# Two gates of a decoder trunk: three 256-column products per weight tile, one bank per chunk, and a last tile emptied in two halves

## The chip, the cores and the metric

The kernel runs on one core of one Trainium2 chip. A core has a matmul engine (TensorE, PE in the profile, with its weight loads as PEld), a vector engine (VectorE, DVE), a scalar engine (ScalarE, ACT), a general one (GpSimd, POOL) and a queue for transfers (SyncE, SP). The metric is device time in microseconds (us). Three runs of the kernel before took 669.51, 670.52 and 673.18 us; the median is 670.52.

## What is computed

Two layers of a decoder on 256 tokens with 1024 features, in f32. Each layer has a mixer (attention), a squared-ReLU MLP, and at its end a gate, which is what the change touches:

```python
for i in range(DEPTH):                      # DEPTH = 2
    hn = rms_norm(h, mix_norm[i])
    h = h + mixer_i(hn)                     # even or odd mixer
    u = jax.nn.relu(rms_norm(h, ff_norm[i]) @ w_ff1[i])
    h = h + (u * u) @ w_ff2[i]
    g = jax.nn.sigmoid(rms_norm(h, ple_norm[i]) @ w_ple_gate[i])
    h = h + g * (p[i] @ w_ple_proj[i])
return h
```

## The kernel before

The residual `h` lies in SBUF with features on the partitions: 8 row tiles of 128 features by 256 tokens. A `Norm` object holds the input of a product: row tiles of `h` times the norm's gain, split into a high part (`hi`, rounded for a fast matmul mode, made by ScalarE, L248) and a low rest (`lo`, VectorE, L249). The factor 1/rms of a token isn't in it: it is found beside the product from the sum of squares (`square`, `cols`) and multiplied in at the end, as `rb` in the gate.

Weights come in 1 MB tiles, in the order of `plan`, into three buffers (`raw`). Each tile is split in four pieces into `hi` (ScalarE, L182) and `lo` (VectorE, L184), ahead of its use. These pieces have a low priority for the scheduler that orders each engine's instructions (`LATER`), and it sets them between the other work of ScalarE and VectorE. A product is then three: high by high, low x by high weight, high x by low weight.

A gate has 4 chunks of 256 output columns; a chunk is two column tiles of 128, each with 8 row tiles of weights, so a gate has 64 weight tiles. `wide_mm` (L312, L314) takes a weight tile's high part against the 512 columns of [hi | lo] of x, into two halves of a bank, and its low part against the 256 columns of hi. The two halves are added afterwards: a ScalarE copy (L622) and a VectorE addition (L623). Then come the product with `rb` (L624), the sigmoid (L626), the product with the embedding projection (L627), the addition to `h` (L628), and either the split of `h` for the next layer or, at the program's end, a transfer to the output (L630). Other products, such as the output projection, go through `feat_mm` (L299): three matmuls of 256 columns for each weight tile, added up in one place of the bank.

Behind the gate of layer 0 stands the q/k/v projection of layer 1 (`tok_units`, L330): for each of 8 row tiles of x, six matmuls of 512 columns, with x as the loaded operand and four row tiles in a weight tile.

Of the kernel before, what the change touches and what calls it, by code (L numbers as in the profile page):

```python
# [8 lines left out]
F32 = mybir.dt.float32  # L9
FR = mybir.dt.float32r  # L10
I32 = mybir.dt.int32
AF = mybir.ActivationFunctionType
# [3 lines left out]
P = 128  # L16
S = 256
# [4 lines left out]
ZB = 7  # L22
# [30 lines left out]
def trunk(ctx, tc, xT, pT, pos, cst, vec, w_c, w_kv, w_dil, w_uq, w_ukv, w_eo,  # L53
          w_odd, w_oo, w_f1, w_f2, w_g, w_p, out):
    nc = tc.nc
# [6 lines left out]
    tp = ctx.enter_context(tc.tile_pool(name="tp", bufs=2))  # L62
    sp = ctx.enter_context(tc.tile_pool(name="sp", bufs=3))
    pm = ctx.enter_context(tc.tile_pool(name="pm", bufs=4, space=PS))
    pa = ctx.enter_context(tc.tile_pool(name="pa", bufs=2, space=PS))
    pt = ctx.enter_context(tc.tile_pool(name="pt", bufs=2, space=PS))

    V, A, T, G = nc.vector, nc.scalar, nc.tensor, nc.gpsimd
# [4 lines left out]
    h = cp.tile([P, KD, S], F32, name="h")  # L73
# [71 lines left out]
    class Weights:  # L145
# [56 lines left out]
        def take(self, ahead=True):  # L202
            while len(self.ready) <= self.taken or (self.rest and self.rest[0][0] == self.taken):
                self.piece()
            if not self.rest:
                self.flush()
            self.taken += 1
            if ahead:
                self.pump(99)
            return self.ready[self.taken - 1]  # L210

    weights = Weights()
    take, pump = weights.take, weights.pump
# [76 lines left out]
    def passes(xh, xl, wh, wl):  # L290
        return ((wh, xh), (wh, xl), (wl, xh))

    def feat_mm(ps, n, wt, x, k0, nk, total, done):

        (wh, wl), (xh, xl) = wt, x
        for kk in range(nk):
            for j in range(n):
                for i, (a, b) in enumerate(passes(xh, xl, wh, wl)):
                    T.matmul(ps[:, j, :], lhsT=a[:, kk, j * P:(j + 1) * P],  # L299
                             rhs=b[:, k0 + kk, :],  # L300
                             start=(done == 0 and kk == 0 and j == 0 and i == 0),
                             stop=(done + kk == total - 1 and i == 2),
                             skip_group_check=True)

    def wide_mm(ps, j, wt, x, nk, done=True, first=True):


        wh, wl = wt
        sl = slice(j * P, (j + 1) * P)
        for kk in range(nk):  # L310
            last = done and kk == nk - 1
            T.matmul(ps, lhsT=wh[:, kk, sl], rhs=x[:, kk], start=(first and kk == 0),  # L312
                     stop=last, skip_group_check=True)
            T.matmul(ps[:, 0, :], lhsT=wl[:, kk, sl], rhs=x[:, kk, 0, :], start=False,  # L314
                     stop=last, skip_group_check=True)

    def wide_first(pss, wt, x):

        for kk in range(8):
            for j, ps in enumerate(pss):  # L320
                wide_mm(ps, j, (wt[0][:, kk:kk + 1], wt[1][:, kk:kk + 1]), x[:, kk:kk + 1], 1,
                        kk == 7, kk == 0)
# [282 lines left out]
        down(3)  # L605

    def gate(n_g, es, nxt):
        rb = None
        for c in range(4):
            wt = take()  # L610
            pool, tag = (pa, "s") if c == 2 else (pm, "mm")
            pss = [pool.tile([P, 2, S], F32, tag=tag, name="g") for _ in range(2)]
            if c == 0:
                wide_first(pss, wt, n_g.x)
            for j, ps in enumerate(pss):
                k = 2 * c + j
                if c > 0:
                    wide_mm(ps, j, wt, n_g.x, 8)
                if rb is None:
                    rb = n_g.cols()  # L620
                t = tp.tile([P, S], F32, tag="z", name="t", bufs=ZB)
                A.activation(t, ps[:, 1, :], AF.Copy)  # L622
                V.tensor_add(t, ps[:, 0, :], t)  # L623
                V.tensor_mul(t, t, rb)  # L624
                g = tp.tile([P, S], F32, tag="sq", name="g")
                A.activation(g, t, AF.Sigmoid)  # L626
                V.tensor_mul(g, es[k // 4][:, k % 4, :], g)  # L627
                V.tensor_add(h[:, k, :], h[:, k, :], g)  # L628
                if nxt is None:
                    nc.sync.dma_start(out[:, k, :], h[:, k, :])  # L630
                else:
                    nxt.split(k)
            if nxt is not None:
                nxt.square(c)


    def rope_angles():
# [189 lines left out]
    with tc.manual_schedule():  # L827
# [3 lines left out]
        pss = [pm.tile([P, 512], F32, tag="mm", name="mm") for _ in range(2)]  # L831
        wts = [weight_tiles([P, 4, 416]) for _ in range(2)]
        for k in range(8):
# [6 lines left out]
            sl = slice(k % 4, k % 4 + 1)  # L840
# [10 lines left out]
        wh, wl = take(False)  # L851
# [7 lines left out]
        for k in range(8):  # L859
            if k == 4:  # L860
                wh, wl = take(False)
            tok_mm(psk, 256, (wh[:, k % 4:k % 4 + 1], wl[:, k % 4:k % 4 + 1]), x0, k, 1, 8, k)
    with tc.manual_schedule(engines={mybir.EngineType.PE}):
# [46 lines left out]
        es, pss = [], []  # L910
# [29 lines left out]
    mlp(0, nf, ng)  # L940
    n1 = Norm(V_MIX + 8)
    gate(ng, es, n1)


# [32 lines left out]
    with tc.manual_schedule(engines={mybir.EngineType.PE}):  # L977
        run(group(0))
        for g in range(2):
            if g == 0:  # L980
                dense, units = group(1), [3, 3, 3, 3, 3]
            else:
                es, pss = [], []
# [8 lines left out]
    ng = Norm(V_PLE + 8)  # L992
    mlp(1, nf, ng)
    gate(ng, es, None)


# [86 lines left out]
```

## Time and profile before

| | |
|---|---|
| median of three runs | 670.52 us |
| profiled execution | 670.03 us |
| its span, first to last instruction | 668.0 us |
| TensorE busy | 653.2 us (98%) |
| VectorE busy | 524.5 us (79%) |
| ScalarE busy | 471.9 us (71%) |
| mean granted TensorE clock | 0.998 |
| gate of layer 0 | about 310.0 to 333.2 us |
| gate of layer 1 | about 639.3 to 662.5 us |

The shares are means over the whole span. The ends of matmuls are modelled, so the distance from start to start tells what one costs. An engine that isn't on the path may be slower or faster without effect; it matters where another engine waits for it.

### The profile page before, as it was taken

To read this page: it belongs to the slowest core of one execution; us is meant where nothing else is said; L and a number is where in the kernel's file an instruction comes from. 1 tells how busy PE (TensorE), PEld (TensorE's weight loads), DVE (VectorE), ACT (ScalarE), POOL (GpSimd) and SP (SyncE) were. 2 spreads that over 40 slices of the span, in tenths; PEclk is the share of its full clock that TensorE was granted. 3 is DMA by queue.
4 is the path that set the end of the run, shared out by engine and by line. 5 is a ranking of instruction groups with operands and counts; after the bars stand their busy time and mean duration, and the time that the engine had idled before them with its cause. 6 is when DMAs were issued, how large, how long until landed. Compare 5 with 4: busy or idle time off the path is not lost.

```text
span 668.0 us, 10798 instructions
## 1 busy us (share of the span) xinstructions
PE 653.2 (98%) x3862; PEld 564.3 (84%) x3862; DVE 524.5 (79%) x1307; ACT 471.9 (71%) x1118; POOL 12.9 (2%) x38
## 2 busy tenths in 40 slices
PE   9999999999999999999989999999999999999996
PEld 8888778988888888888868777888888888888885
DVE  5799787697787787889988686666977878778996
ACT  6968886599858658557864775766986585785663
POOL 3110000000000000000000000000000000000000
PEclk9999999999999999999999999999999999999999
DMA  7756413156546455455345433331754564554511
GB/s 232 277 195 243 181 64 127 64 178 240 191 164 219 163 190 217 164 177 187 119 189 212 172 130 138 121 127 64 266 199 173 186 213 171 211 187 172 187 57 63
DMA packets 19493, 114.08 MB, mean 171 GB/s; under 512 B 2288, under 2 KB 5488, under 8 KB 6640
## 3 DMA queue, kind: packets, MB, share of 16 engines
q1 hardware_dynamic: 19440, 113.40, 47.8%
q8 instruction: 30, 0.49, 0.3%
q14 instruction: 23, 0.19, 0.1%
HBM read 112.34 MB, written 1.05 MB: 170 GB/s over the span
## 4 chain that ended last, share of the span: by engine, by line
PE 88%; DVE 7%; ACT 2%; DMA 2%; issue 1%; SPq 1%; ACTq 0%
PE f L312 34%; PE f L314 18%; PE mm L330 16%; PE mm L299 7%; PE g L312 3%; PE g L314 2%; PE tr L419 2%; DVE lo L184 1%; DVE x L249 1%; PE tr L339 1%; PE s L389 1%; PE o L428 1%; PE s L387 1%; DMA raw<-w_kv 1%; DVE acc L260 1%
## 5 line engine op out<-in xcount | busy, mean ns | idle before, releaser
L184 DVE TENSOR_TENSOR lo<-raw,hi 128x512 fp32r<-128x512 f32 (+1 forms) x400 | 266.2, 690 | 57.5 <-ACT hi L182 57.1
L182 ACT ACTIVATE hi<-raw 128x512 fp32r<-128x512 f32 (+1 forms) x400 | 234.8, 629 | 100.9 <-PE f L312 60.7
L312 PE MATMUL f<-x,hi 128*128 128x512 f32 x512 | 178.3, 392 | 0.0
L312 PE MATMUL f<-u,hi 128*128 128x512 f32 x512 | 177.8, 391 | 0.0
L314 PE MATMUL f<-x,lo 128*128 128x256 f32 x512 | 143.4, 280 | 0.0
L314 PE MATMUL f<-u,lo 128*128 128x256 f32 x512 | 143.4, 280 | 0.0
L312 PEld LDWEIGHTS f<-x,hi 128*128 128x128 f32 x512 | 95.8, 187 | 21.3
L312 PEld LDWEIGHTS f<-u,hi 128*128 128x128 f32 x512 | 95.7, 187 | 21.0
L330 PE MATMUL mm<-hi,x 128*128 128x512 f32 (+1 forms) x320 | 105.5, 398 | 0.2 <-ACT hi L121 0.2
L314 PEld LDWEIGHTS f<-x,lo 128*128 128x128 f32 x512 | 96.8, 189 | 0.0
L314 PEld LDWEIGHTS f<-u,lo 128*128 128x128 f32 x512 | 96.8, 189 | 0.0
L330 PEld LDWEIGHTS mm<-hi,x 128*128 128x128 f32 x320 | 61.1, 191 | 13.5 <-issue 1.8
L330 PE MATMUL mm<-lo,x 128*128 128x512 f32 (+1 forms) x160 | 63.2, 395 | 3.3 <-DVE lo L184 3.3
L299 PE MATMUL mm<-x,hi 128*128 128x256 f32 x256 | 48.3, 289 | 0.0
L576 DVE TENSOR_TENSOR u<-sq,u 128x256 fp32r<-128x256 f32 x64 | 26.7, 420 | 26.7 <-ACT u L575 26.7
L312 PE MATMUL g<-x,hi 128*128 128x512 f32 x128 | 44.5, 392 | 0.0
L299 PEld LDWEIGHTS mm<-x,hi 128*128 128x128 f32 x256 | 39.5, 190 | 3.7 <-issue 3.0
L330 PEld LDWEIGHTS mm<-lo,x 128*128 128x128 f32 x160 | 30.6, 191 | 10.3 <-DVE lo L184 4.2
L314 PE MATMUL g<-x,lo 128*128 128x256 f32 x128 | 36.2, 283 | 0.0
L299 PE MATMUL mm<-x,lo 128*128 128x256 f32 x128 | 36.1, 282 | 0.0
L248 ACT ACTIVATE x<-h,vc 128x256 fp32r<-128x256 f32 x48 | 22.8, 501 | 14.3 <-DVE h L595 9.6
L401 ACT ACTIVATE pr<-sc,nm 128x128 f32<-128x128 f32 x64 | 27.5, 447 | 7.4 <-DVE nm L396 7.3
(195 smaller groups left out, 843.6 us busy)
## 6 DMA issues: line engine op xcount, KB each, us to landing
raw<-w_f SPq DMA_DIRECT2D x64, 1024.0 KB, 4.7
raw<-w_odd SPq DMA_DIRECT2D x12, 1024.0 KB, 4.7
raw<-w_g SPq DMA_DIRECT2D x8, 1024.0 KB, 4.7
raw<-w_dil SPq DMA_DIRECT2D x6, 1024.0 KB, 4.9
raw<-w_eo SPq DMA_DIRECT2D x4, 1024.0 KB, 4.8
raw<-w_oo SPq DMA_DIRECT2D x4, 1024.0 KB, 5.0
raw<-w_p SPq DMA_DIRECT2D x2, 1024.0 KB, 4.8
raw<-w_c SPq DMA_DIRECT2D x8, 208.0 KB, 4.2
```

Of the source, the lines that this page charges most:

```text
L182: A.activation(hi, raw, AF.Copy)
L184: self.low = lambda: V.tensor_sub(lo, raw, hi.bitcast(F32))
L248: A.activation(self.hi[:, k, :], h[:, k, :], AF.Copy, scale=g)
L249: V.scalar_tensor_tensor(self.lo[:, k, :], h[:, k, :], g, self.hi[:, k, :].bitcast(F32), op0=OP.mult, op1=OP.subtract)
L260: V.tensor_add(self.acc, self.acc, sq)
L299: T.matmul(ps[:, j, :], lhsT=a[:, kk, j * P:(j + 1) * P], rhs=b[:, k0 + kk, :], start=(done == 0 and kk == 0 and j == 0 and i == 0), stop= ...
L312: T.matmul(ps, lhsT=wh[:, kk, sl], rhs=x[:, kk], start=(first and kk == 0), stop=last, skip_group_check=True)
L314: T.matmul(ps[:, 0, :], lhsT=wl[:, kk, sl], rhs=x[:, kk, 0, :], start=False, stop=last, skip_group_check=True)
L330: T.matmul(pss[t][:, :n], lhsT=a[:, k0 + kk, t * P:(t + 1) * P], rhs=b[:, kk, :], start=(done + kk == 0 and i == 0), stop=(done + kk == to ...
L401: A.activation(prs[i][:, sl], scs[i][:, sl], AF.Exp, scale=-1.0, bias=nms[i][:, t:t + 1], **kw)
L419: T.transpose(ps[:, i * P:(i + 1) * P], pr[:, i * P:(i + 1) * P], ident)
L576: V.tensor_sub(ul, sq, uh.bitcast(F32))
```

## The change

Both gates call `feat_mm` with both column tiles of a chunk in one bank, so the high and low products are added by TensorE itself. Copy and addition fall away; product with `rb`, sigmoid, product and addition to `h` run once per chunk on 512 elements of a partition. The split for the next layer follows per chunk (`pair`). In the last gate the fourth chunk is done tile by tile, and its second tile is emptied in two halves of 128 tokens, each with its own transfer.

```diff
     def gate(n_g, es, nxt):
+        x = (n_g.hi, n_g.lo)
         rb = None
         for c in range(4):
-            wt = take()
-            pool, tag = (pa, "s") if c == 2 else (pm, "mm")
-            pss = [pool.tile([P, 2, S], F32, tag=tag, name="g") for _ in range(2)]
-            if c == 0:
-                wide_first(pss, wt, n_g.x)
-            for j, ps in enumerate(pss):
-                k = 2 * c + j
-                if c > 0:
-                    wide_mm(ps, j, wt, n_g.x, 8)
+            wh, wl = take()
+            last = c == 3 and nxt is None
+            for a, b in ((0, 1), (1, 2)) if last else ((0, 2),):
+                n = b - a
+                sl = slice(a * P, b * P)
+                pool, tag = (pa, "s") if c % 2 else (pm, "mm")
+                ps = pool.tile([P, 2, S], F32, tag=tag, name="g")[:, :n, :]
+                feat_mm(ps, n, (wh[:, :, sl], wl[:, :, sl]), x, 0, 8, 8, 0)
                 if rb is None:
-                    rb = n_g.cols()
-                t = tp.tile([P, S], F32, tag="z", name="t", bufs=ZB)
-                A.activation(t, ps[:, 1, :], AF.Copy)
-                V.tensor_add(t, ps[:, 0, :], t)
-                V.tensor_mul(t, t, rb)
-                g = tp.tile([P, S], F32, tag="sq", name="g")
-                A.activation(g, t, AF.Sigmoid)
-                V.tensor_mul(g, es[k // 4][:, k % 4, :], g)
-                V.tensor_add(h[:, k, :], h[:, k, :], g)
-                if nxt is None:
-                    nc.sync.dma_start(out[:, k, :], h[:, k, :])
-                else:
-                    nxt.split(k)
+                    rb = n_g.cols()[:, None, :]
+                halves = ((0, P), (P, S)) if last and a else ((0, S),)
+                for u, v in halves:
+                    t = tp.tile([P, 2, S], F32, tag="z", name="t", bufs=ZB)[:, :n, :v - u]
+                    V.tensor_mul(t, ps[:, :, u:v], rb[:, :, u:v].to_broadcast([P, n, v - u]))
+                    g = tp.tile([P, 2, S], F32, tag="sq", name="g")[:, :n, :v - u]
+                    A.activation(g, t, AF.Sigmoid)
+                    k = 2 * (c % 2) + a
+                    V.tensor_mul(g, es[c // 2][:, k:k + n, u:v], g)
+                    hp_ = h[:, 2 * c + a:2 * c + b, u:v]
+                    V.tensor_add(hp_, hp_, g)
+                    if nxt is None:
+                        nc.sync.dma_start(out[:, 2 * c + a:2 * c + b, u:v], hp_)
             if nxt is not None:
-                nxt.square(c)
+                nxt.pair(c)
```

The scheduler's order on VectorE changes with it. At the end of layer 0's gate it was this before (lo_3874 is the low part of layer 1's first weight tile, lo_3943 of its second; g, t and h are the gate's, x_3723 is layer 1's input):

```order
L628 TENSOR_TENSOR h_84<-h_84,g_3933 128x256
L249 SCALAR_TENSOR_TENSOR x_3723<-h_84,vc_82,x_3723 128x256
L623 TENSOR_TENSOR t_3998<-g_3955,t_3998 128x256
L184 TENSOR_TENSOR lo_3874<-raw_3728,hi_3873 128x512
L249 SCALAR_TENSOR_TENSOR x_3723<-h_84,vc_82,x_3723 128x256
L260 TENSOR_TENSOR acc_3724<-acc_3724,sq_3939 128x512
L627 TENSOR_TENSOR g_3976<-ple_1082,g_3976 128x256
L624 TENSOR_TENSOR t_3998<-t_3998,cr_3774 128x256
L628 TENSOR_TENSOR h_84<-h_84,g_3976 128x256
L184 TENSOR_TENSOR lo_3943<-raw_3807,hi_3942 128x512
L627 TENSOR_TENSOR g_4002<-ple_1082,g_4002 128x256
L249 SCALAR_TENSOR_TENSOR x_3723<-h_84,vc_82,x_3723 128x256
```

Two rows further on there, behind another L628, stands the last piece of lo_3874. Now the third chunk's work (t_3944, g_3946) reads as follows, with lo_3884 as the low part of layer 1's first weight tile and lo_3958 of its second:

```order
L184 TENSOR_TENSOR lo_3884<-raw_3728,hi_3883 128x512
L249 SCALAR_TENSOR_TENSOR x_3723<-h_84,vc_82,x_3723 128x256 x2
L184 TENSOR_TENSOR lo_3884<-raw_3728,hi_3883 128x512
L249 SCALAR_TENSOR_TENSOR x_3723<-h_84,vc_82,x_3723 128x256 x2
L260 TENSOR_TENSOR acc_3724<-acc_3724,sq_3880 128x512
L624 TENSOR_TENSOR t_3944<-g_3895,cr_3789 128x512
L184 TENSOR_TENSOR lo_3884<-raw_3728,hi_3883 128x512
L184 TENSOR_TENSOR lo_3958<-raw_3812,hi_3957 128x512
L628 TENSOR_TENSOR g_3946<-ple_1082,g_3946 128x512
L184 TENSOR_TENSOR lo_3884<-raw_3728,hi_3883 128x512
L630 TENSOR_TENSOR h_84<-h_84,g_3946 128x512
L184 TENSOR_TENSOR lo_3958<-raw_3812,hi_3957 128x512 x2
```

All four pieces of layer 1's first weight tile now stand ahead of the third chunk's addition to `h`, where the last of them stood behind the last chunk's. On ScalarE, at the last chunk of the same gate, the order is now this (hi_4048 is the high part of layer 1's third weight tile, g_4020 the last chunk's sigmoid):

```order
L248 ACTIVATE x_3723<-h_84,vc_82 128x256 x2
L259 ACTIVATE sq_3954<-h_84 128x512
L182 ACTIVATE hi_4048<-raw_3886 128x512 x4
L626 ACTIVATE g_4020<-t_4018 128x512
L248 ACTIVATE x_3723<-h_84,vc_82 128x256 x2
```

The third tile's four pieces stand in front of the last sigmoid. At the program's end VectorE empties the last two column tiles so:

```order
L624 TENSOR_TENSOR t<-g,cr 128x256
L628 TENSOR_TENSOR g<-ple,g 128x256
L630 TENSOR_TENSOR h<-h,g 128x256
L624 TENSOR_TENSOR t<-g,cr 128x128 x2
L628 TENSOR_TENSOR g<-ple,g 128x128 x2
L630 TENSOR_TENSOR h<-h,g 128x128 x2
```

Each step is done for both halves before the next step begins; before, each tile had L623, L624, L627 and L628 on 256 columns.

## Rows read from the trace of the kernel before

**Rows 1.** Busy us by stretch: PE, PEld, DVE, ACT, POOL; clock, DMA share, GB/s:
```profile
310.00:333.20 23.20, 23.20 (x134) 20.37 (x133) 21.58 (x53) 18.54 (x42) 0.00 (x0) 1.00 0.38 136
333.20:340.00 6.80, 3.53 (x16) 2.38 (x14) 6.80 (x18) 5.68 (x14) 0.00 (x0) 1.00 0.00 0
639.30:662.50 23.20, 23.19 (x133) 20.09 (x131) 20.27 (x49) 13.03 (x29) 0.00 (x0) 1.00 0.11 35
```
**Rows 2.** Waits of TensorE, whole run: us in total, times, longest:
```profile
PE mm L330 <- DVE lo L184: 3.3, 2, 2.0
```
**Rows 3.** Timeline of TensorE, gate of layer 1 (start, duration), 20 tiles apart:
```profile
646.72 0.40 PE L312 MATMUL g<-x,hi 128*128 128x512 f32 x1
...
653.66 0.39 PE L312 MATMUL g<-x,hi 128*128 128x512 f32 x1
```
**Rows 4.** Timeline of TensorE, output projection of layer 1, 13 tiles apart:
```profile
455.05 0.40 PE L299 MATMUL mm<-x,hi 128*128 128x256 f32 x2
...
459.73 0.40 PE L299 MATMUL mm<-x,hi 128*128 128x256 f32 x2
```
**Rows 5.** Timeline of TensorE, q/k/v projection of layer 1, nine matmuls apart:
```profile
361.02 0.39 PE L330 MATMUL mm<-lo,x 128*128 128x512 f32 x1
...
363.06 0.39 PE L330 MATMUL mm<-lo,x 128*128 128x512 f32 x1
```
**Rows 6.** Groups of VectorE from 310 to 340: busy us, mean ns, idle before:
```profile
L623 DVE TENSOR_TENSOR t<-g,t 128x256 f32<-128x256 f32 x8 | 3.3, 418 | 0.5 <-ACT t L622 0.5
L624 DVE TENSOR_TENSOR t<-t,cr 128x256 f32<-128x256 f32 x8 | 3.2, 418 | 0.0
```
**Rows 7.** Groups of ScalarE from 310 to 340:
```profile
L182 ACT ACTIVATE hi<-raw 128x512 fp32r<-128x512 f32 x20 | 12.2, 630 | 2.5 <-PE g L312 2.1 <-ACT sq L259 0.5
...
L626 ACT ACTIVATE g<-t 128x256 f32<-128x256 f32 x8 | 3.2, 414 | 0.0
L622 ACT ACTIVATE t<-g 128x256 f32<-128x256 f32 x8 | 3.0, 378 | 1.2 <-PE g L314 1.2
```
**Rows 8.** Timeline of VectorE around the end of layer 0's gate:
```profile
321.95 1.09 DVE L624 TENSOR_TENSOR t<-t,cr 128x256 f32<-128x256 f32 x3
...
334.89 0.68 DVE L184 TENSOR_TENSOR lo<-raw,hi 128x512 fp32r<-128x512 f32 x1
...
339.17 1.28 DVE L184 TENSOR_TENSOR lo<-raw,hi 128x512 fp32r<-128x512 f32 x2
```
**Rows 9.** Timeline of TensorE at the start of layer 1, waits in brackets:
```profile
333.23 0.39 PE L330 MATMUL mm<-hi,x 128*128 128x512 f32 x1
335.63 0.50 PE L330 MATMUL mm<-lo,x 128*128 128x512 f32 x1 [2.01 <-DVE lo L184]
...
339.90 0.50 PE L330 MATMUL mm<-lo,x 128*128 128x512 f32 x1 [1.26 <-DVE lo L184]
```
**Rows 10.** Timeline of ScalarE in layer 1's first projection:
```profile
344.72 0.63 ACT L182 ACTIVATE hi<-raw 128x512 fp32r<-128x512 f32 x1 [4.41 <-DMA raw<-w_odd]
```
**Rows 11.** Timeline of SyncE in layer 0's gate (weights of layer 1):
```profile
312.57 9.86 SPq L156 DMA_DIRECT2D raw<-w_odd  x3
```
**Rows 12.** Chain that ended last, its final part (start, us):
```profile
662.37 0.13 PE g L314
...
662.59 0.39 ACT t L622
...
664.83 0.42 DVE h L628
```
**Rows 13.** Output transfers: issue ns (min/median/max), first and last start; time to landing:
```profile
L630 SPq DMA_DIRECT2D outT<-h x8: 332/333/431, 654.7 to 665.3; - x8
...
DMA to landing us min/median/max: 1.9/1.9/2.0
```
**Rows 14.** Groups of VectorE, whole run, 128 columns out of PSUM:
```profile
L773 DVE TENSOR_TENSOR rp<-mm,rs 128x128 f32<-128x128 f32 x4 | 1.1, 280 | 0.0
```
**Rows 15.** Groups of ScalarE, whole run, exponentials of 128 columns:
```profile
L401 ACT ACTIVATE pr<-sc,nm 128x128 f32<-128x128 f32 x32 | 12.6, 395 | 7.3 <-DVE nm L396 7.3
```

## The prediction

> **What bounds the kernel now.** I read the busy time by stretch first: in both gates TensorE is busy for the whole 23.2 us [rows 1], so an instruction added there is paid for in full. Then the list of what TensorE waited for: its longest line by far is 3.3 us in two waits for the low weight halves that VectorE makes (L184) [rows 2]. The timeline puts both waits right behind the gate of layer 0, in the first matmuls of layer 1 [rows 9]. VectorE had no free time there, busy for 21.6 of the gate's 23.2 us and for all of the 6.8 behind it [rows 1]; the pieces that TensorE waited for started at 334.89 and 339.17, behind gate work [rows 8]. Last the chain at the end of the program: from the last matmul's end at 662.50 six instructions follow one by one until 665.25, then an output transfer [rows 12, 13]. So three places count: the pitch of the gate's matmuls (128 weight tiles, 64 in each gate), the 3.3 us at the border of the layers, and the tail.
>
> **The gate's matmuls: +1.7 us.** Before, a weight tile takes a matmul of 512 columns and one of 256; 20 tiles go from 646.72 to 653.66, 0.347 us each [rows 3]. After, it takes three of 256 columns by L299. The output projection does just this already: 13 tiles from 455.05 to 459.73, 0.360 us each, or 0.120 for one matmul [rows 4]. Nine matmuls of 512 columns take 2.04 us, 0.227 each [rows 5]. Together: 256 columns cost 0.107 us and each matmul 0.013 us beside its columns; the old tile (768 columns, two matmuls) comes to 0.347 and the new one to 0.360, as measured. 128 tiles by 0.013 us is +1.7, 0.85 in each gate, all on the path. Bounds: nothing (the old pitch) and 0.120 - 0.107 doubled, 3.4 us; I take the row of the same code.
>
> **The wait behind gate 0: -3.3 us.** What goes: of each column tile one ScalarE copy (L622) and one VectorE addition (L623), eight of each in a gate [rows 6, 7]; what is left runs once per chunk on 512 elements. VectorE's 256-wide operations follow each other at 0.335 us (three take 1.09, the last of them 0.42), its 512-wide ones at 0.60 (two take 1.28, the last 0.68) [rows 8]. A chunk cost 8 by 0.335 = 2.7 us and will cost 3 by 0.60 = 1.8; four chunks save 3.5 us of an engine that was nearly full. ScalarE loses eight copies of 0.378 us, and pairs of sigmoids become single ones of at most 0.83 us (twice 0.414) [rows 7]. No time is gained by that as such: VectorE isn't on the path inside the gate. It counts because of what stands behind it. In the old order the last low piece of layer 1's first weight tile (lo_3874) stands behind the last chunk's last addition; in the new one (lo_3884) before the addition of the third chunk.
>
> The times, estimated: the gate holds 64 tiles and 1.0 us of other matmuls (23.2 - 64 by 0.347). From 310.0 the third chunk ends on TensorE at 310.0 + 48 by 0.360 + 1.0 = 328.3. VectorE then does the product with the row factor (it may be a microsecond late with it), two low pieces, the product with the embedding after the sigmoid, and the last wanted piece: five by 0.60 and about a microsecond of lateness, 331.4 to 332.4. TensorE comes to layer 1 at 333.2 + 0.85 = 334.1. Slack some 2 us, so both waits go whole. Bounds: 0 (as long as before) and 3.3.
>
> What is late next: the last chunk is finished as a whole, so rows 6 and 7 of x come later than before. ScalarE's four pieces ahead of the sigmoid need a buffer that TensorE frees at the gate's end; the sigmoid ends near 336.9, the two VectorE operations with three low pieces between and beside them near 339.3, the scaling and the low halves of x near 341.4. TensorE wants row 6 at 334.1 + 36 by 0.227 = 342.3. This slack of 0.9 us is the thinnest. The second weight tile's pieces end at 337, wanted at 334.1 + 24 by 0.227 = 339.5. In gate 1 nothing follows that could wait; its chunks' work lies beside TensorE's until the last tile.
>
> The first chunk's bank is held until the row factor is there, since the copy out of it is gone. But a gate takes two banks of the pool of four now, where it took six, and no matmul of the gate comes back to that one: no cost.
>
> **The tail: -1.0 us.** Before, 662.50 to 665.25: copy, addition, product, sigmoid, product, addition, each on 256 columns [rows 12]. After: product, sigmoid, product, addition in two halves of 128 columns. A 128-wide VectorE operation takes 0.28 us [rows 14] and, by the difference to 256 columns, 0.2 to the next; the half sigmoid 0.31 (0.414 less half the difference of a wide and a narrow one, my estimate; at most the 0.395 of the exponentials of that width [rows 15]). From the end of the last matmul: products done at 0.38 and 0.59, sigmoids at 0.72 and 0.92, products at 1.03 and 1.24, additions at 1.44 and 1.65. The first transfer is issued at 1.46, and an issue takes 0.33 [rows 13], so the second begins at 1.79, against 2.8 before (665.3). Landing takes 1.9 whichever of the eight it is, and I leave it so for half a tile. -1.0; bounds -0.6 (issue and landing of the second half 0.4 slower) and -1.3.
>
> **The sum.** The profiled execution took 670.03 us, its span 668.0. +1.7 - 3.3 - 1.0 = -2.6, so 667.4. The median of the three runs, 670.52, is 0.5 above it and would give 667.9; I say 667.7. It is a gain of 0.4%; a measurement of this kernel tells about 0.5%, 3.4 us, from no change.
>
> **Rivals.**
> A: a matmul more costs nothing, the engine being held by columns alone. Then the gates keep 0.347 a tile: 670.0 - 3.3 - 1.0 = 665.7, by the median 666.2; I say 666.0. For it: columns are the same 768. Against it: the 0.360 of the same code [rows 4], in a stretch without waits. The Trainium skill (TensorE: Matmul & The Clock Gate, "Back-to-back issue gap") gives a gap of the columns over 2.4 GHz and 2.5 ns, by which a third matmul adds 2.5 ns to a tile and 0.3 us to the program, almost this case; the trace has 13 ns.
>
> B: VectorE's freed time goes elsewhere, or row 6 of x is late: 1 to 3.3 us of wait come back, 668.7 to 671.0. For it: the slack of 0.9 us rests on a chain of some ten estimates. Against it: no piece of the first two weight tiles is near its due time.
>
> C, slower: a transfer of weights gets ahead of the last chunk. ScalarE works in order, and four high pieces (hi_4048) of the third weight tile now stand ahead of the last sigmoid. ScalarE has waited 4.41 us for such a tile, until 344.72 [rows 10]. Should this be the tile that comes then, four pieces of 0.63 [rows 7] and a sigmoid end at 344.7 + 2.5 + 0.8 = 348.0 rather than 336.9, row 6 of x is there some 11 us later, at 352.5, and TensorE stands 10 us: 678. It decides from a landing later than about 335. Against it: before, the issues of the first three layer-1 tiles were through at 322.4 [rows 11], and a landing takes 5 us (the piece that frees the buffer ends at 339.85, data at 344.72 [rows 8, 10]); the late one was the fourth. In the new order the third tile's buffer is freed no later than about 320.
>
> **How the numbers follow.** Forecast 0.68, A 0.10, B 0.15, C 0.07. 80% lie from 665.8 (A) to 670.8 (nearly all of B); C is outside. Faster by over 0.5% begins below 667.2: A, and a quarter of the forecast's own spread (666.5 to 668.9), 0.27. Slower is C, 0.07. The rest, 0.66, cannot be told from no change.
>
> **What would show it.** In the profile after: L299's matmuls of g at 0.12 us from start to start, a gate of 24.0 us; no line of L330 waiting for L184 among TensorE's waits; VectorE idle for some time in the gates; the last transfer issued about 1.8 us behind the last matmul. Wrong: gates of 23.2 us (A), waits of L330 for x or for L184 behind gate 0 (B), ScalarE's sigmoid behind a transfer (C).

## The result, and the profile after

The kernel after takes 666.33 us, median of five executions (666.08 to 666.69), beside 670.04 for the kernel before in the same session; the ratio is 0.9937, interval 0.9916 to 0.9959. The forecast was 667.7. One thing must be known to read any whole time here: in every profile but e10's, each of the two MLP blocks takes either 179.1 or 182.4 us, and which it is can change from execution to execution of one kernel (after and e11 are the same kernel; shown below, with e10). So times come some 3.3 us apart, and I compare stretches inside the traces; both profiles of before and after hold the short length twice. Seven executions of the later sessions took 802 to 1654 us, and no ratio or group below uses them.

The profiled execution after took 666.69 us, its span 664.9; before 670.03 and 668.0. By stretch, in us, each read from the starts on TensorE's timeline:

| stretch | before | after | difference | forecast |
|---|---|---|---|---|
| start to gate of layer 0 | 310.09 | 309.95 | -0.14 | 0 |
| gate of layer 0 | 23.14 | 24.10 | +0.96 | +0.85 |
| layer 1's first matmul to its statistics (L272) | 14.84 | 10.90 | -3.94 | -3.3 |
| statistics to MLP, and MLP of layer 1 | 291.11 | 291.15 | +0.04 | 0 |
| gate of layer 1, to the last matmul's end | 23.31 | 24.27 | +0.96 | +0.85 |
| tail, to the end of the span | 5.54 | 4.56 | -1.0 | -1.0 |

The differences add up to -3.1, the difference of the spans; the other 0.2 lies outside the span (2.03 us before, 1.79 after). It is not scatter: in the session of e11 it is 1.95 to 2.07 us in every execution of before and 1.74 to 1.82 in every one of after. Its cause stays open.

Busy time in three stretches of after, the columns of [rows 1]:

```profile
309.95:334.05 24.10, 24.10 (x199) 23.84 (x198) 22.13 (x42) 17.63 (x35) 0.00 (x0) 1.00 0.39 135
334.05:344.95 10.90, 10.90 (x50) 9.02 (x49) 10.27 (x19) 8.43 (x15) 0.00 (x0) 1.00 0.76 282
636.10:660.38 24.28, 24.26 (x198) 23.79 (x196) 17.46 (x33) 10.36 (x19) 0.00 (x0) 1.00 0.10 36
```

TensorE now has no idle time behind gate 0 (10.90 of 10.90), where it was busy for 3.53 of 6.8 [rows 1]. VectorE is still nearly full in gate 0 (22.13 of 24.10): the time that the gate's work no longer takes went to low pieces, not to idling. In the gate of layer 1, with nothing behind it, it has 6.8 us free, where it had 2.9 [rows 1].

What TensorE waited for in the whole run after, the top of the list, answering [rows 2]:

```profile
PE warm L81 <- DVE gc L866: 1.0, 1, 1.0
PE kv L330 <- DVE lo L184: 0.8, 2, 0.5
PE st L285 <- DVE acc L260: 0.8, 2, 0.4
```

The line of 3.3 us is gone; the longest is now a warm-up. The start of layer 1 on TensorE, answering [rows 9], with two of the gate's rows ahead of it, 11 weight tiles apart:

```profile
329.73 0.40 PE L299 MATMUL g<-x,hi 128*128 128x256 f32 x2
...
333.69 0.40 PE L299 MATMUL g<-x,hi 128*128 128x256 f32 x2
333.93 0.28 PE L299 MATMUL g<-x,lo 128*128 128x256 f32 x1
334.05 0.40 PE L330 MATMUL mm<-hi,x 128*128 128x512 f32 x1
334.28 0.40 PE L330 MATMUL mm<-lo,x 128*128 128x512 f32 x1
```

3.96 us for 11 tiles are 0.360 each, as in [rows 4]; the second matmul of layer 1 follows the first by 0.23 where it took 2.40 [rows 9]. VectorE (answering [rows 8]) and then ScalarE at this place:

```profile
322.73 0.69 DVE L624 TENSOR_TENSOR t<-g,cr 128x512 f32<-128x512 f32 x1 [0.91 <-PE g L299]
323.33 1.48 DVE L628 TENSOR_TENSOR g<-ple,g 128x512 f32<-128x512 f32 x2
...
329.92 1.29 DVE L184 TENSOR_TENSOR lo<-raw,hi 128x512 fp32r<-128x512 f32 x2
...
331.72 0.69 DVE L184 TENSOR_TENSOR lo<-raw,hi 128x512 fp32r<-128x512 f32 x1
...
340.34 0.88 DVE L249 SCALAR_TENSOR_TENSOR x<-h,vc,x 128x256 fp32r<-128x256 f32 x2
```

```profile
334.39 2.18 ACT L182 ACTIVATE hi<-raw 128x512 fp32r<-128x512 f32 x4
336.47 0.61 ACT L626 ACTIVATE g<-t 128x512 f32<-128x512 f32 x1
```

VectorE waits 0.91 us for TensorE at 322.73, inside the gate: it has caught up. The low piece of 331.72 ends at 332.41, 1.9 us before TensorE needs any (334.28). The last sigmoid of the gate ends at 337.08, the low halves of rows 6 and 7 of x at 341.22.

The tail, answering [rows 12]; the last matmul ends at 660.36. Then the issues of the output transfers and their times to landing, answering [rows 13], by size:

```profile
660.40 0.49 DVE L624 TENSOR_TENSOR t<-g,cr 128x128 f32<-128x128 f32 x2 [1.08 <-PE g L299]
660.73 0.51 ACT L626 ACTIVATE g<-t 128x128 f32<-128x128 f32 x2 [2.32 <-DVE t L624]
661.07 0.50 DVE L628 TENSOR_TENSOR g<-ple,g 128x128 f32<-128x128 f32 x2 [0.18 <-ACT g L626]
661.48 0.49 DVE L630 TENSOR_TENSOR h<-h,g 128x128 f32<-128x128 f32 x2
661.79 0.81 SPq L632 DMA_DIRECT2D outT<-h  x2
```

```profile
outT<-h SPq DMA_DIRECT2D x3, 256.0 KB, 2.2
outT<-h SPq DMA_DIRECT2D x1, 128.0 KB, 1.9
outT<-h SPq DMA_DIRECT2D x2, 64.0 KB, 1.7
```

The additions end at 661.97, 1.61 us behind the last matmul (before: 665.25, 2.75 behind). The first transfer is issued 1.43 us behind it, the second 1.86 (at 662.22), when the first issue is through.

### The profile page after: what moved, and what is told of

It is laid out like the page before. It is cut to its first block, busy times and chain, and to the rows that moved or that the text cites. A ratio compares the mean times of both kernels' runs of the same rounds, so it can differ in the third digit from the quotient of the medians.

```text
span 664.9 us, 10993 instructions
## 1 busy us (share of the span) xinstructions
PE 653.2 (98%) x3990; PEld 567.6 (85%) x3990; DVE 518.4 (78%) x1273; ACT 466.6 (70%) x1096; POOL 12.4 (2%) x38
## 3 DMA queue, kind: packets, MB, share of 16 engines
HBM read 112.34 MB, written 1.05 MB: 171 GB/s over the span
## 4 chain that ended last, share of the span: by engine, by line
PE 90%; DVE 5%; DMA 2%; ACT 1%; issue 1%; SPq 1%; DVEq 0%
PE f L312 34%; PE f L314 17%; PE mm L330 16%; PE mm L299 7%; PE g L299 7%; PE tr L419 2%; PE tr L339 1%; PE s L389 1%; PE o L428 1%; DVE lo L184 1%; PE s L387 1%; DMA raw<-w_kv 1%; DVE x L249 1%; PE kv L330 1%; DMA h<-xT 1%
## 5 line engine op out<-in xcount | busy, mean ns | idle before, releaser
L299 PE MATMUL g<-x,hi 128*128 128x256 f32 x256 | 47.0, 285 | 0.0
L299 PEld LDWEIGHTS g<-x,hi 128*128 128x128 f32 x256 | 40.0, 192 | 0.5 <-DVE x L249 0.3
```

Of the source, the lines that this page charges most:

```text
L299: T.matmul(ps[:, j, :], lhsT=a[:, kk, j * P:(j + 1) * P], rhs=b[:, k0 + kk, :], start=(done == 0 and kk == 0 and j == 0 and i == 0), stop= ...
```

## The experiments

The stretches of all profiles, in us ("to statistics" is from layer 1's first matmul to its statistics, the tail from the last matmul's end to the end of the span), with the median of all executions of each kernel (which mixes the lengths of the MLPs):

| kernel | MLP 0 | gate 0 | to statistics | MLP 1 | gate 1 | tail | span | median |
|---|---|---|---|---|---|---|---|---|
| before | 179.10 | 23.14 | 14.84 | 179.09 | 23.3 | 5.54 | 668.0 | 670.04 |
| after | 179.10 | 24.10 | 10.90 | 179.09 | 24.3 | 4.56 | 664.9 | 666.33 |
| e1 | 182.39 | 24.10 | 10.91 | 182.38 | 23.3 | 5.55 | 671.0 | 670.29 |
| e2 | 179.10 | 23.13 | 14.84 | 179.09 | 24.3 | 4.56 | 667.8 | 672.65 |
| e3 | 182.39 | 24.10 | 12.95 | 179.08 | 24.3 | 5.55 | 671.1 | 673.23 |
| e4 | 182.39 | 23.19 | 12.38 | 179.09 | 23.6 | 5.56 | 669.5 | 670.68 |
| e5 | 182.39 | 24.11 | 10.91 | 179.09 | 24.3 | 4.82 | 668.2 | 671.4 |
| e6 | 182.40 | 24.10 | 10.91 | 182.39 | 24.3 | 4.61 | 671.7 | 669.81 |
| e7 | 179.09 | 24.11 | 10.91 | 179.08 | 24.3 | 4.41 | 664.4 | 671.34 |
| e8 | 182.39 | 23.59 | 10.91 | 182.39 | 23.7 | 4.56 | 670.9 | 671.71 |
| e9 | 179.09 | 23.56 | 10.91 | 182.38 | 23.5 | 4.41 | 666.5 | 668.21 |
| e10 | 179.92 | 23.59 | 11.13 | 179.92 | 23.6 | 4.39 | 664.6 | 666.81 |
| e11 | 179.09 | 24.09 | 10.91 | 182.39 | 24.3 | 4.56 | 667.8 | 669.58 |

The medians of before beside them were 673.56 (e1 to e4), 676.12 (e5 to e8) and 673.28 (e9 to e11).

**e1 and e2: one gate at a time.**

```diff
-    gate(ng, es, n1)
+    gate_new(ng, es, n1)      # e1; in e2 the old gate
...
-    gate(ng, es, None)
+    gate_old(ng, es, None)    # e1; in e2 the new gate
```

> Only the gate of layer 0 is changed, the last gate is as before. Theory (three separate terms that add up: matmul pitch +0.95 us in a gate, the two waits behind gate 0, the tail): span 668.0 + 0.95 - 3.9 = 665.0 us, no wait of L330 for L184 left. The 3.9 is the stretch from layer 1's first matmul to its statistics, 14.84 us before and 10.90 after, so a wait costs some 0.3 us more than the idle time that the profile lists for it. Rival 1 (a wait costs its listed idle time, 3.3, and the other 0.6 us came from elsewhere): 665.6. Rival 2 (the gain is mostly in the last gate and its tail): 667 or more.

> Only the last gate is changed. Theory: +0.95 for its matmuls and -1.0 for the tail, span 667.9 to 668.1, and the waits of 3.3 us behind gate 0 stay. Rival (the last gate gains by itself, its emptying being on the path more than the tail shows): 667.0 or less.

Measured: the whole times mix the lengths of the MLPs and did not answer (ratios 0.997, 0.9949 to 0.9990, and 1.0001, 0.997 to 1.0031), and e1's profile drew the long MLP twice. The stretches do: e1 has +0.96 in gate 0 and -3.93 behind it, -2.97 in all; e2 has +0.96 in gate 1 and -1.0 in the tail, nothing in all. The two parts are independent, and the gain is that of gate 0 alone: in gate 1 the third matmul costs what the new tail gives.

**e3: three products only,** the epilogue as before (copy, addition, each column tile by itself), in both gates.

```diff
-                    wide_mm(ps, j, wt, n_g.x, 8)
+                    three_mm(ps, j, wt, n_g.x, 8)
...
+            for i, (w, half, dst) in enumerate(((wh, 0, 0), (wh, 1, 1), (wl, 0, 0))):
+                T.matmul(ps[:, dst, :], lhsT=w[:, kk, sl], rhs=x[:, kk, half, :], ...)
```

> The matmuls alone: three of 256 columns per weight tile in both gates, but high and low sums in two halves of a bank as before, with the copy, the addition and all work per column tile as before. Theory for the matmuls: both gates 0.9 us longer (24.1 us each). Rival (columns alone count): 23.2 us each. For the waits behind gate 0: if they hang on how much VectorE has to do, they stay at some 3 us and the span is 669.8; if they hang on where the scheduler sets the low pieces (in this kernel it sets all four of layer 1's first tile ahead of the last chunk's work, with the same work on VectorE), they are gone and the span is 665.9.

The start of layer 1 on TensorE in e3:

```profile
337.20 0.39 PE L330 MATMUL mm<-hi,x 128*128 128x512 f32 x1
339.30 0.50 PE L330 MATMUL mm<-lo,x 128*128 128x512 f32 x1 [1.70 <-DVE lo L184]
```

Both gates are as long as after's (24.10 and 24.3), so their length is the third matmul and nothing else of the change. One of the two waits is left, and the stretch takes 12.95, so neither branch of the expectation held. Of the 1.89 us less than before, 0.96 is only TensorE's later arrival: from the start of gate 0 to the statistics it is 37.05 us against 37.98 before and 35.00 after. That is 0.93 of 2.98 us, and the third matmul of gate 1 costs as much again: for the whole program the products alone bring nothing.

**e4: copy and addition left out, the old products, each column tile still by itself,** in gate 0.

```diff
-                A.activation(t, ps[:, 1, :], AF.Copy)
-                V.tensor_add(t, ps[:, 0, :], t)
-                V.tensor_mul(t, t, rb)
+                V.tensor_mul(t, ps[:, 0, :], rb)
```

> In the gate of layer 0 the copy L622 and the addition L623 are left out, so the product of the high weights with the low part of x is computed and not added; all else is as before, the old matmuls too. VectorE has 2.7 us less to do there. Theory (the waits come from VectorE's load and cost 3.9 with their restart): gate 0 keeps 23.2 us, waits gone or under 0.5, span 664.1 to 664.6. Rival 1 (listed idle time only): 664.7 to 665.2. Rival 2 (not the load, but the chunk-wide order of the new gate takes the waits away): waits stay at about 3, span 668.

TensorE in e4, layer 1's first matmuls and the one wait that is left:

```profile
336.78 0.39 PE L330 MATMUL mm<-hi,x 128*128 128x512 f32 x1
337.01 0.40 PE L330 MATMUL mm<-lo,x 128*128 128x512 f32 x1
...
342.30 0.61 PE L330 MATMUL mm<-hi,x 128*128 128x512 f32 x2
343.77 0.50 PE L330 MATMUL mm<-lo,x 128*128 128x512 f32 x1 [0.85 <-DVE lo L184]
```

The first wait is gone without the eight copies and additions; a second, 7.0 us into the layer, stays, and the stretch takes 12.38. Of the 1.48 us more than after's 10.90, 0.91 is only TensorE's earlier arrival (gate 0 takes 23.19 and not 24.10). Counted from the start of gate 0, as for e3, it is 35.57 us, against 37.98 before and 35.00 after: leaving out copies and additions, with the order that the scheduler then chose, is worth 2.41 of the 2.98, and 0.57 is left. Two things can make it up, and no run separates them: the load that e4 still has more (six operations of 256 columns a chunk at 0.335 are 2.0 us, three of 512 at 0.60 are 1.8 [rows 8]), and the arrangement, one epilogue a chunk letting the pieces of the second weight tile in earlier. Of the recorded theories none held: a wait of 0.85 is neither under 0.5 nor about 3. Order alone was not run by itself.

**e5 to e7: the tail.** All are the kernel after with one edit in the last tile. e5:

```diff
-                halves = ((0, P), (P, S)) if last and a else ((0, S),)
+                halves = ((0, S),)
```

e6 (one transfer behind both halves) and e7 (the second half's issue on another queue):

```diff
-                        nc.sync.dma_start(out[..., u:v], hp_)
+                nc.sync.dma_start(out[..., :], h[..., :])              # e6
...
+                        q = nc.scalar if u else nc.sync                # e7
+                        q.dma_start(out[..., u:v], hp_)
```

> The kernel after, but the program's last tile is emptied whole: one product, sigmoid, product and addition of 256 columns and one output transfer. My theory: the halves gain nearly nothing. Their work ends 1.60 us behind the last matmul, but the second half's transfer is issued only when the first issue is through, at about 1.85; whole, the four steps of 256 columns end at about 1.80 (0.45 to the next) and the one transfer is issued then. So the tail, from the end of the last matmul to the end of the span, stays at 4.5 us, within 0.15. Rival: the halves carry the gain of the tail, a shorter chain; then the tail is 4.9 or more. The rest of the program as in the kernel after: gates 24.1, 10.9 from layer 1's first matmul to its statistics.

> The kernel after with the last tile still computed in halves, but written by one transfer behind both. My theory (the second issue queues behind the first on SyncE's queue): the one transfer is issued at 1.62 us behind the last matmul rather than about 1.85 and the tail is 4.2 to 4.35 us, 0.2 to 0.3 shorter than after's 4.5. Rival: a transfer of 128 KB lands later than one of 64 (1.9 against 1.7 in the kernel after), which takes it all back: 4.45 to 4.55.

> The kernel after, but the second half's output transfer is issued on ScalarE's queue, so that it does not stand behind the first half's issue. My theory: it is issued at about 1.62 us behind the last matmul, lands in 1.7, and the tail is 4.2 to 4.3 us against 4.5. Rival: what an issue costs on ScalarE, or a second queue that the program's end waits for, is as much: 4.5 or more.

The last addition and the issue in e5 (last matmul's end 663.40), in e6 (667.05) and the two issues in e7 (659.95), each from its own timeline:

```profile
664.81 0.42 DVE L630 TENSOR_TENSOR h<-h,g 128x256 f32<-128x256 f32 x1
665.26 0.33 SPq L632 DMA_DIRECT2D outT<-h  x1
```

```profile
668.16 0.49 DVE L630 TENSOR_TENSOR h<-h,g 128x128 f32<-128x128 f32 x2
668.68 0.33 SPq L632 DMA_DIRECT2D outT<-h  x1
```

```profile
661.38 0.33 SPq L633 DMA_DIRECT2D outT<-h  x1
661.58 0.37 ACTq L633 DMA_DIRECT2D outT<-h  x1
```

The steps were as expected: whole, the one issue starts 1.86 us behind the last matmul; halves with one transfer, 1.63; on two queues, the second at 1.63 too. The tails were not: 4.82, 4.61 and 4.41 against after's 4.56. In e5 neither theory held (within 0.15 of after, or 0.4 more): it lost 0.26. What both left out is the size of the transfer. The last issue starts at 1.86, 1.63, 1.63 and in after at 1.86 again; add the landing by size, 1.9, 1.9, 1.8 (its row in e7, on ScalarE's queue) and 1.7, and the end of the program is 1.0 to 1.1 us behind the landing in all four. So halving the columns of the compute gains 0.23 and halving the transfer 0.2, and the queue in between takes the 0.23 back: after's last issue starts no earlier than e5's, and what the halves gain comes with the smaller last transfer. e6's first theory fell, its rival is nearer. e7 gains 0.15, between its theory (4.2 to 4.3) and its rival (4.5 or more). The gain is no accident of one profile: e9 and e10, with the same two queues, have tails of 4.41 and 4.39, and e2, e8 and e11, with one, have 4.56. (The 4.53 and 4.45 in the expectation of e9 came from spans given to 0.1 us.)

**e8: the old products where their epilogue has room** (chunks 0 and 1 of gate 0, 0 to 2 of gate 1), the chunk's epilogue otherwise as after.

```diff
+                wide = c < (2 if nxt is not None else 3)
...
+                if wide:
+                    ps = tp.tile([P, 2, S], F32, tag="z", name="t", bufs=ZB)
+                    for j in range(2):
+                        A.activation(ps[:, j, :], pss[j][:, 1, :], AF.Copy)
+                        V.tensor_add(ps[:, j, :], pss[j][:, 0, :], ps[:, j, :])
```

> The kernel after, but chunks 0 and 1 of the gate of layer 0 and chunks 0 to 2 of the gate of layer 1 take the old matmuls (512 and 256 columns a weight tile, the ScalarE copy and a VectorE addition for each column tile, the rest per chunk). 80 of 128 weight tiles go back to the old pitch. My theory: 0.015 us each, so gate 0 takes 23.6 us instead of 24.1 and gate 1 0.7 less than after; the four additions more on VectorE lie in the first half of gate 0, where the wanted low pieces are 2 to 3 us early, so the 10.9 us behind the gate stay. In all 1.2 us less than after, with both MLPs at their shorter length of 179.1 us a span of 663.7. Rival: the freed VectorE time was needed: the stretch behind gate 0 grows to 11.5 us or more, and the gain is half or nothing.

Measured: gate 0 takes 23.59, gate 1 23.7, and the 10.91 behind gate 0 stay: 1.05 us less than after, of 1.2 expected. The rival fell; four additions more on VectorE cost nothing there. So it is not the amount of work in the gate alone that counts: here the work in its first half was free. The shortfall is in gate 1, whose old tiles ran at 0.353 in this execution and not 0.347.

**e9 to e11: the best of these, the length of the MLPs, and after once more.** e9 is e8 and e7 together, e11 the kernel after unchanged; e10 is e9 with this:

```diff
-            T.matmul(ps, lhsT=wh[:, kk, sl], rhs=x[:, kk], ...)
-            T.matmul(ps[:, 0, :], lhsT=wl[:, kk, sl], rhs=x[:, kk, 0, :], ...)
+            for i in ((0, 1), (1, 0))[kk % 2]:    # i = 0: the wide one, 1: the narrow one
```

> The mixed gates (old products for chunks 0 and 1 of gate 0 and chunks 0 to 2 of gate 1) together with the second half's output transfer on ScalarE's queue. Each measured alone before: the gates 0.51 and 0.55 us shorter than after's, the tail 4.45 us against 4.53, 10.9 us behind gate 0 unchanged. My theory: they add, 1.1 us less than the kernel after in the same length of the MLPs. Rival: one of the two is lost in company, 0.6 or less.

> The same as the mixed gates with two queues, and in every run of old products (512 and 256 columns a weight tile, the MLPs too) the two matmuls change places in every other tile: wide, narrow, narrow, wide. In the runs so far each MLP took either 179.1 or 182.4 us, 346.7 or 353.3 ns a weight tile, and kept its level from the statistics matmuls near its start to its end. Theory 1: the longer level is a matter of how a wide matmul follows a narrow one, so the other order changes it: one length only, or others than these two. Theory 2: the level is set by the moment at which TensorE starts again behind the statistics, whatever the order: 179.1 and 182.4 again.

> The kernel after unchanged, beside the two others on the same chip. Theory: by stretch as before (gates 24.1 and 24.3, 10.9 behind gate 0, tail 4.5), and its MLPs, on this chip, at 179.1 or 182.4 us each, so times near 666.3, 669.6 and 672.9. Rival: the kernel after holds the shorter length of both MLPs in every execution, as in its first five, and the difference to the kernel before is then larger than 3.1 us where that one draws the longer.

The two MLP blocks by busy time (columns as in [rows 1]), in the kernel before, in e1, and in e10:

```profile
130.99:310.09 179.10, 178.72 (x1031) 157.19 (x1030) 144.81 (x308) 132.61 (x309) 0.00 (x0) 1.00 0.53 188
460.09:639.18 179.09, 178.72 (x1031) 157.19 (x1029) 144.77 (x308) 132.61 (x309) 0.00 (x0) 1.00 0.53 188
```

```profile
130.30:312.69 182.39, 182.01 (x1031) 157.63 (x1029) 144.98 (x308) 132.75 (x309) 0.00 (x0) 1.00 0.52 185
459.72:642.10 182.38, 182.01 (x1030) 157.58 (x1029) 144.90 (x308) 132.65 (x309) 0.00 (x0) 1.00 0.52 185
```

```profile
130.14:310.06 179.92, 179.54 (x1030) 156.33 (x1029) 149.16 (x308) 131.17 (x309) 0.00 (x0) 1.00 0.53 188
456.78:636.70 179.92, 179.55 (x1031) 156.34 (x1030) 149.11 (x308) 131.17 (x309) 0.00 (x0) 1.00 0.53 188
```

The matmuls' starts in such a stretch, 20 weight tiles apart, in before, in e1 and in e10:

```profile
199.50 0.39 PE L312 MATMUL f<-x,hi 128*128 128x512 f32 x1
...
206.43 0.39 PE L312 MATMUL f<-x,hi 128*128 128x512 f32 x1
```

```profile
199.62 0.40 PE L312 MATMUL f<-x,hi 128*128 128x512 f32 x1
...
206.69 0.40 PE L312 MATMUL f<-x,hi 128*128 128x512 f32 x1
```

```profile
199.76 0.63 PE L314 MATMUL f<-x,hi 128*128 128x512 f32 x2
...
206.72 0.62 PE L314 MATMUL f<-x,hi 128*128 128x512 f32 x2
```

That is 0.3535 us a tile in e1 and 0.348 in e10, where before has 0.347. TensorE is busy throughout at the same granted clock (1.00, the level of 2.4 GHz), with as many instructions, and yet before and e1 are 3.3 us apart. In e10 both blocks take 179.92, and six executions of it lie from 666.54 to 667.18, while e11 has times of 666.5 (two), 669.3 to 670.1 (seven) and 673.2 to 673.3 (two). So theory 1 holds for the order of the matmuls, as far as one profile and six executions tell: with the new order the two lengths are gone. Why the old order has two was not settled. e9's gains added up (gates 0.53 and 0.7 shorter than e11's, tail 0.15), 1.4 us where 1.1 was expected: its shortest executions are 664.77 and 665.02. By median on this chip e10 is the best, 666.81 against 668.21 (e9), 669.58 (e11) and 673.28 (before); ratio to before 0.9905, interval 0.9867 to 0.9943. With equal MLPs e9 would be the shorter.

e11 also bears out the size of the change. Executions of before and after in that session fall into three groups each: 669.4 to 670.7 and 666.5 to 666.6; 672.3 to 674.0 and 669.3 to 670.1; 676.2 to 677.1 and 673.2 to 673.3. Group by group the kernel after is some 3 to 3.5 us shorter. Its first five executions were all of the shortest group; here it has the others too, so e11's rival fell.

## Why the prediction was right, and where its sizes were off

The direction and the three terms were right, and the time lay in the range, 1.4 us under the forecast: past the bound of 0.5%, to which only 0.27 had been given. No step of the mechanism failed; the term of the wait was mis-sized.

- **The gate's matmuls, +1.7: measured +1.92.** The pitch came as read from the same code: 0.360. Rival A (a third matmul free) fell, with gates of 24.1 and 24.3 here and in e3. The Trainium skill (TensorE: Matmul & The Clock Gate, "Back-to-back issue gap") would have given 2.5 ns for the extra matmul, by its gap for an isolated one; the trace has 13. The other 0.1 us a gate is not in the pitch, and I have not placed it.
- **The wait behind gate 0, -3.3: measured -3.94.** This is the term that was mis-sized, and its upper bound was wrong with it. The prediction took the listed wait for its whole cost. The list counts from the modelled end of the matmul ahead, 0.39 us behind its start, though the next could follow at 0.23; and the first matmul behind a wait takes 0.34 to the next instead of 0.23. From [rows 9] and the two rows between: 335.63 - 333.23 - 0.23 + 0.11 = 2.28 for the one, 339.90 - 338.03 - 2 by 0.227 + 0.11 = 1.53 for the other, 3.8 of the 3.94. A wait costs about a quarter of a microsecond more than its line says. The two rows between, the first behind the first wait and the second ahead of the second:

```profile
335.97 0.62 PE L330 MATMUL mm<-hi,x 128*128 128x512 f32 x2
338.03 0.61 PE L330 MATMUL mm<-hi,x 128*128 128x512 f32 x2
```

- **Where the slack is:** the last low piece was forecast for 331.4 to 332.4 and ended at 332.41; the sigmoid for 336.9, and ended at 337.08; the scaled x for 341.4, and ended at 341.22. The thinnest step held, so rival B did not come, and the sigmoid stood behind no transfer (C).
- **The reason for the vanished wait** was given as load and order together. e4 shows the first: leaving out the copies and additions is worth 2.41 of the 2.98 us from the start of gate 0 to the statistics. That the order gives the last 0.57 is argued and not shown. In e3, with three products and the old load, 2.05 of the 2.98 stay.
- **The tail, -1.0: measured -1.0.** First issue forecast at 1.46 us, measured 1.43; second 1.79 and 1.86. But "landing takes 1.9 whichever" was wrong: 1.7 for half a tile, 2.2 for two tiles. That the sum still came out is in part luck: the landing is 0.2 shorter than assumed, the last issue 0.07 later, and the end of the span stands 1.0 us behind the last landing, where it stood 0.9 before.
- **The chances.** The terms' sum left the forecast 0.5 us short of the bound, and I put the time half-way to a median that held one long MLP (673.18). Both errors, a wait taken at its listed length and a median taken as one population, pushed the same way. Of the 1.4 us, the stretches make 0.5 (the wait -0.64, the matmuls +0.22, the start -0.14), the time outside the span 0.2, the way to the median 0.3; the last 0.4 is that the profiled execution after is the longest of its five.

## What to carry to other kernels

A stall is priced from the starts of the instructions around it, against the pitch of an undisturbed stretch, not from the list of waits. An engine without idle time can still release another, if work is taken off it and what the other waits for stands ahead of the rest; what the freed time is worth shows behind the stage, at the first consumer. Two variants are compared from a common start, not from the arrival of the engine that waits: one that arrives later waits less. Where one program's times come in groups, compare stretches of the traces, and only then medians.

## What the runs showed of the hardware

- A stretch of 512- and 256-column matmuls in turn runs at 346.7 or 353.3 ns a pair (means over 60 pairs), at one granted clock (1.00); it takes one of the two behind the statistics matmuls near its start and keeps it for all of an MLP. Behind the statistics of the gate it takes one anew: in e4 the MLP of layer 1 has 346.7 and its gate 353.1, in e1 353.3 and 347.0. At 2.4 GHz (worked out) that is 832 or 848 clock periods for 768 columns; three matmuls of 256 take 864, so a matmul comes to its columns and 32 periods, and the long level to 16 more for the pair. In turn the other way round in every second pair (e10) it is 348.3 ns, in both blocks.
- Landing of an output transfer: 1.7, 1.9 and 2.2 us for 64, 128 and 256 KB. The Trainium skill (DMA: Bandwidth & Descriptors, "Anatomy of one DMA — SWDGE (gpsimd) path") gives a fixed part of about 2.0 us and bytes beside it for transfers issued from GpSimd, a path that no output transfer here takes; from SyncE's queue 64 KB land in 1.7.
